# Streamed weights laid out tile by tile in memory, so that a load reads one 8 KB run per partition

## The chip, the core and the metric

The kernel runs on one core of a Trainium2 chip. A core has TensorE (matrix products; its weight loads are listed apart as PEld), VectorE (DVE), ScalarE (ACT), GpSimd (POOL) and SyncE (SP), which here only issues DMAs. Sixteen DMA engines move data between the chip's memory and the core's buffers (SBUF, 128 partitions). The metric is device microseconds from start to end of one launch. Laying out the inputs on the host is done before the launch and is not timed.

## What is computed

Four layers over 256 tokens of 1024 channels, all in float32. The first block has two layers: a mixer (hybrid of a gated recurrence and sparse attention, then latent attention) and an MLP with a gated side input. The second block has two layers: three mixers side by side (retention, RWKV-7, short convolution), then a mixture of 32 experts with two chosen per token. Cut to what matters for the weights:

```python
for i in range(2):                                   # first block
    m = hybrid_mixer(x, hy_w_in, ..., hy_w_out) if i == 0 else mla_mixer(x, mla_w_down, ..., mla_w_out)
    h = layer_norm(alpha * x + m)
    f = square(relu(h @ mlp_w1[i])) @ mlp_w2[i]
    e = sigmoid(h @ ple_w_gate[i]) * (p[i] @ ple_w_proj[i])
    x = layer_norm(alpha * h + f + e)
for l in range(2):                                   # second block
    x = x + gate1 * (mixers(modulate(rms_norm(x)), w_in[l], w_gate[l], w_branch[l]) @ w_o[l])
    x = x + gate2 * sum over the chosen experts e of
        weight[e] * ((silu(h @ w_exp_gate[l, e]) * (h @ w_exp_up[l, e])) @ w_exp_down[l, e])
```

An expert has three matrices: gate and up of 1024 x 512, down of 512 x 1024, 2 MB each. All 32 experts of a layer are read, 192 MB per layer.

## The kernel before

Activations lie with their channels on the partitions, 256 tokens along each. Weights stream through tiles of [128, 2048] float32, 1 MB, one DMA each. A dense tile is a block of `kc` times 128 rows and 2048 / `kc` columns; it is read by `wload` (L291 to L295) out of the matrix as it stands, so that each partition gets `kc` runs of 2048 / `kc` floats: 8 runs of 1 KB for most matrices, 4 of 2 KB or 2 of 4 KB for some. `wsplit` (L297 to L306) then copies half of such a tile into its high float32r part on ScalarE (L302) and forms the rest on VectorE or GpSimd (L305), and `mm3` makes three products of these parts (L318 to L320). `gemm_steps` runs a whole product so. The modulation weights w_ada are used as they come (L1091).

The experts (L1883 to L1902) use their matrices without parts. `xload` (L1730 to L1738) reads a matrix in two halves: gate and up in 4 runs of 2 KB per partition and half, down in 2 runs of 4 KB. Its tiles come in turn from three pools (`xtile`, L1720): 7 of the experts' ring (xw), the 7 of the dense weights (w) and 3 of a second ring, 17 in all; a load waits until the tile 17 loads earlier has been used. In step e the TensorE makes the gate product of expert e (L1758), the down product of expert e - 1 (L1782), the up product of e (L1758), adds the outputs of e - 1 to the tokens' sums (`combine`, L1923), then `choice` (L1746 on TensorE, L1749 on ScalarE, L1751 on VectorE) and `expert_act`: ScalarE L1765, VectorE L1767, two transposes L1770 on TensorE, VectorE L1772. The choice gives the weight that L1767 needs. Every fourth expert the tokens of four more experts are gathered (L1839). Behind the last expert all engines pass a branch (L1933), which is for expert lists of over 64 tokens.

All loads of weights are issued by SP in one queue, in an order that is fixed when the kernel is built, as is the order on each engine: a planner lays the instructions of the expert loop out by its own estimate of when each can start, except where the code has them in the written order (`ordered`, `manual_schedule`). At the start (L172 to L177) x and the first two weight tiles are loaded in turn: two parts of x in 1 KB runs, two halves of the first tile in runs of 512 bytes, the second tile in 1 KB runs.

Of the kernel before, what the change touches and what calls it, by code (L numbers as in the profile page):

```python
# [20 lines left out]
T = 256  # L21
# [5 lines left out]
# ---------------------------------------------------------------- host layout  # L27
# per-channel vectors, packed as columns of [128, n]
# [16 lines left out]
# shape constants, packed as columns of [128, n]  # L45
# [10 lines left out]
def constants():  # L56
# [23 lines left out]
    # block doubling of (I + A)^-1: rows t (partition), columns s; level b joins blocks of 2^b  # L80
# [10 lines left out]

def layout(a):
    """The arrays that the program reads, of the inputs: only moved, repeated and padded."""
# [4 lines left out]
    g["xT"] = a["x"][0].T  # L98
    g["pT"] = np.transpose(a["p"][:, 0], (0, 2, 1))
    w = a["hy_w_in"][0]  # L100
    xr, yr, q, k, v, iq, ik, iw = np.split(w, np.cumsum([512, 512, 512, 64, 64, 256, 64])[:7], axis=1)
    g["hy_w_in"] = np.concatenate(
        [iq, ik, ik, v, iw, np.zeros((1024, 60), np.float32), k, k, q, xr, yr], axis=1)
    for n in ("hy_ga_w", "hy_gx_w"):
# [5 lines left out]
    g["hy_w_out"] = a["hy_w_out"][0]  # L110
# [3 lines left out]
    g["mla_w_down"] = np.concatenate([w[:, 512:768], *[kr] * 4, *[krot] * 4, w[:, :512]], axis=1)  # L114
    w = a["mla_w_uq"][0].reshape(512, 16, 96)
    # the rotary parts of heads whose logits share a bank lie on the same partitions
# [4 lines left out]
    g["mla_w_uq"] = np.concatenate([x[:, i] for i in range(2) for x in (n, r, rot)], axis=1)  # L121
    w = a["mla_w_ukv"][0].reshape(256, 16, 128)
    g["mla_w_ukv"] = np.concatenate(
        [w[:, :, :64].reshape(256, 1024), w[:, :, 64:].reshape(256, 1024)], axis=1)
    g["mla_w_out"] = a["mla_w_out"][0]
    for n in ("mlp_w1", "mlp_w2", "ple_w_proj", "ple_w_gate"):
        g[n] = a[n]
# [3 lines left out]
    # four groups, four that are never chosen, the experts  # L131
# [4 lines left out]
    for n in ("w_ada", "w_in", "w_gate", "w_branch", "w_o", "w_exp_gate", "w_exp_up", "w_exp_down"):  # L136
        g[n] = a[n + "_2"]
# [17 lines left out]
class Prog:  # L155
    def __init__(self, ctx, tc, g, out):
# [13 lines left out]
        # x and the first weights in turn  # L170
        w, w1 = (self.wp.tile([128, 2048], FT, name="w", tag="w").rearrange("p (c n) -> p c n", c=8) for _ in range(2))
        self.first = [w, w1]  # L172
# [32 lines left out]
    def enter(self, phase):  # L205
        """The pools of a phase: products with parts of dense weights, or experts."""
# [63 lines left out]
    def t4(self, name, dt=FT, tag="t4"):  # L270
        """An activation of up to 1024 numbers in a partition."""
# [18 lines left out]
    # ---- products with streamed weights, three passes of exact float32r parts  # L290
    def wload(self, ap, k0, kc, c0, n):  # L291
        t = self.wp.tile([128, 2048], FT, name="w", tag="w")
        v = t[:, :kc * n].rearrange("p (c n) -> p c n", c=kc)
        self.nc.sync.dma_start(v, ap[k0:k0 + kc * 128, c0:c0 + n].rearrange("(c p) n -> p c n", p=128))
        return v  # L295

    def wsplit(self, v, kc, c0, n, fresh=False, pool=False):  # L297
        nc = self.nc
        src = v[:, :, c0:c0 + n]
        h = self.t4("fh", FR) if fresh else self.sp.tile([128, 1024], FR, name="wh", tag="wh")  # L300
        hv = h[:, :kc * n].rearrange("p (c n) -> p c n", c=kc)
        nc.scalar.activation(hv, src, AF.Copy)  # L302
        l = self.t4("fl", FR) if fresh else self.sp.tile([128, 1024], FR, name="wl", tag="wl")
        lv = l[:, :kc * n].rearrange("p (c n) -> p c n", c=kc)
# [3 lines left out]
    def split(self, src, h, l):  # L308
        """src = h + l in float32r parts; src may be in PSUM."""
# [3 lines left out]
    def mm3(self, out, wh, wl, wc, xh, xl, kc, x0=0, start=True, stop=True, ks=None):  # L313
        """out[128 columns wc.., T] += w^T x"""
# [11 lines left out]
    def gemm_steps(self, ap, kc, c0, nblk, x, evac, fresh=False, pool=(), first=None):  # L326
        """evac(j, n, bank) for each pair of blocks of 128 columns: bank[:, :n*T] = (x @ w)^T;
        fresh: x comes chunk by chunk, and the first pair of blocks takes each as it comes,
        after a first step that prepares this"""
        tb = 2048 // kc // 128  # L330
        xb = max(1, 1024 // kc // 128)
        for j in range(0, nblk, tb):
            nb = min(tb, nblk - j)
            v = first.pop(0) if first else self.wload(ap, 0, kc, c0 + j * 128, nb * 128)
            parts = {}
            for i in range(0, nb, 2):
                n = min(2, nb - i)
                if fresh and i + j == 0:
                    ws = [self.wsplit(v, kc, u * 128, 128, True) for u in range(2)]
# [9 lines left out]
                for u in range(n):  # L349
                    b = i + u  # L350
                    if b // xb not in parts:
                        w = min(xb, nb - b)
                        parts = {b // xb: self.wsplit(v, kc, b * 128, w * 128, pool=(j + b) % 4 in pool)}
# [29 lines left out]
    def beside(self, main, side):  # L383
        """the steps of side, between those of main, which yields how many units are to come; both results"""
# [34 lines left out]
    def rstd_tokens(self, sq, n, eps, fill=lambda n: None, units=0, out=None):  # L419
        """1 / sqrt(mean of n chunks + eps): [128 tokens, 2]"""  # L420
# [4 lines left out]
    def rstd_sums(self, sums, n, eps, out=None):  # L425
        """the same of what `partial` has summed in PSUM"""
# [14 lines left out]
    def by_token(self, r):  # L441
        """[128 tokens, 2] as [128, T] with all of it on every partition (in PSUM)"""
# [5 lines left out]
    def rstd(self, sq, n, eps, fill=lambda n: None, units=(0, 0)):  # L448
        """1 / sqrt(mean of n chunks + eps) by token, on every partition (in PSUM)"""
# [4 lines left out]
    def rms(self):  # L454
        """1 / rms(x) [128 tokens, 2]"""
# [51 lines left out]
    # ---- first block  # L507
# [11 lines left out]
    def softmax_pair(self, lg, n, scale, hs=2):  # L519
        """lg: PSUM [128, hs, n] logits / scale -> normalised P in SBUF [128, hs, n]"""  # L520
# [1595 lines left out]
```

## Time and profile before

| | |
|---|---|
| median of 3 runs | 2482.08 us (2476.62 to 2482.94) |
| span of the profiled execution | 2477.0 us; no other time of that execution is given |
| TensorE busy | 2295.0 us, 93% |
| VectorE, ScalarE, GpSimd busy | 46%, 35%, 8% |
| DMA | 658.71 MB in 409219 packets, mean 266 GB/s |
| packets under 2 KB, under 8 KB | 234544, 409008 |

A packet is one run that a DMA engine moves. Times are in microseconds from the start of the span unless marked ns. The page cuts the span into 40 equal slices of 61.9 us; a digit is a busy share in tenths. The DMA share is the packets' time over that of 16 engines; it passes 1 where the times of packets overlap. Waits are put down to what ended them.

### The profile page before, as it was taken

The numbers are of one execution on the slowest core, as the hardware profiler recorded it, in microseconds if no ns is written. First come the engines' busy times: TensorE is split into PE (matmuls) and PEld (weight loads), VectorE is DVE, ScalarE is ACT, GpSimd is POOL, SyncE is SP. The second block draws the span as 40 slices with busy tenths as digits, with TensorE's granted clock in tenths as the row PEclk, the third lists the DMA queues.
The fourth block names the chain that finished last, engine by engine and source line by source line (L and its number), as shares of the span: only waits on it lengthen the run. The fifth ranks groups of instructions, "written<-read, shape, count | busy, mean of one in ns | idle before, by whom it ended". The sixth has DMA issues, their size and how long they took to land. (4 is left out here: it accounts for less than half of the span.)

```text
span 2477.0 us, 45869 instructions
## 1 busy us (share of the span) xinstructions
PE 2295.0 (93%) x19846; PEld 1807.9 (73%) x19846; DVE 1144.9 (46%) x1864; ACT 869.2 (35%) x1415; POOL 200.2 (8%) x171
## 2 busy tenths in 40 slices
PE   7899999999999999989899988799999898998886
PEld 7689988799988898975555544389989755554443
DVE  6775566665555855652222211268556522222112
ACT  4654445554445434431111111253344411121111
POOL 6110000010001001010000000010011100000000
PEclk9999999999999999999999999999999999999998
DMA  8855565755567443569999999964335599999996
GB/s 275 266 186 187 181 209 198 238 172 187 181 203 243 151 134 112 184 241 363 394 393 393 394 394 394 366 213 154 121 121 195 204 374 394 394 393 394 394 394 254
DMA packets 409219, 658.71 MB, mean 266 GB/s; under 512 B 10416, under 2 KB 234544, under 8 KB 409008
## 3 DMA queue, kind: packets, MB, share of 16 engines
q1 hardware_dynamic: 407024, 652.14, 74.4%
q8 instruction: 159, 2.61, 0.4%
q10 hardware_dynamic: 1984, 3.54, 0.4%
q14 instruction: 52, 0.43, 0.0%
HBM read 654.59 MB, written 1.05 MB: 265 GB/s over the span
## 5 line engine op out<-in xcount | busy, mean ns | idle before, releaser
L302 ACT ACTIVATE wh<-w 128x1024 fp32r<-128x1024 f32 x359 | 380.4, 1060 | 561.7 <-PE bank L319 493.0
L305 DVE TENSOR_TENSOR wl<-w,wh 128x1024 fp32r<-128x1024 f32 x330 | 420.1, 1274 | 333.1 <-ACT wh L302 332.2
L318 PE MATMUL bank<-hh,wh 128*128 128x256 f32 x1568 | 454.3, 290 | 0.0
L320 PE MATMUL bank<-hh,wl 128*128 128x256 f32 x1568 | 444.4, 283 | 3.6 <-DVE wl L305 3.6
L319 PE MATMUL bank<-hl,wh 128*128 128x256 f32 x1568 | 444.0, 283 | 0.0
L318 PEld LDWEIGHTS bank<-hh,wh 128*128 128x128 f32 x1568 | 300.7, 192 | 11.2 <-issue 7.9
L1758 PE MATMUL bank<-xw,xg 128*64 128x256 f32 x2464 | 286.4, 382 | 21.6 <-DMA xw<-in_w_exp_up_dram 19.7
L320 PEld LDWEIGHTS bank<-hh,wl 128*128 128x128 f32 x1568 | 301.1, 192 | 5.0 <-DVE wl L305 5.0
L319 PEld LDWEIGHTS bank<-hl,wh 128*128 128x128 f32 x1568 | 301.2, 192 | 1.1 <-issue 1.0
L1758 PEld LDWEIGHTS bank<-xw,xg 128*64 128x64 f32 x2464 | 170.9, 137 | 136.8 <-DMA xw<-in_w_exp_up_dram 36.1
L1788 DVE TENSOR_TENSOR ey<-bank,ey 64x512 fp32r<-64x512 f32 x128 | 88.2, 689 | 263.3 <-ACT ey L1787 263.3
L1758 PE MATMUL bank<-w,xg 128*64 128x256 f32 x1632 | 191.1, 382 | 13.0 <-DMA w<-in_w_exp_up_dram 12.4
L1758 PEld LDWEIGHTS bank<-w,xg 128*64 128x64 f32 x1632 | 112.7, 137 | 89.5 <-DMA w<-in_w_exp_up_dram 23.4
L1787 ACT ACTIVATE ey<-bank 64x512 fp32r<-64x512 f32 x128 | 75.9, 593 | 268.2 <-PE bank L1782 220.5
L1751 DVE TENSOR_SCALAR ct<-cs 128x256 fp32r<-128x256 f32 x64 | 20.2, 316 | 324.0 <-ACT cs L1749 324.0
L1782 PE MATMUL bank<-xw,eh 128*64 128x512 f32 x608 | 143.6, 598 | 9.8 <-DMA xw<-in_w_exp_down_dram 8.6
L1749 ACT ACTIVATE cs<-bank 128x256 f32<-128x256 f32 x64 | 24.6, 384 | 363.3 <-PE bank L1746 363.3
L318 PE MATMUL bank<-rh,wh 128*128 128x256 f32 x512 | 144.9, 283 | 0.0
L319 PE MATMUL bank<-rl,wh 128*128 128x256 f32 x512 | 144.9, 283 | 0.0
L320 PE MATMUL bank<-rh,wl 128*128 128x256 f32 x512 | 144.9, 283 | 0.0
L1782 PE MATMUL bank<-w,eh 128*64 128x512 f32 x416 | 98.3, 598 | 9.7 <-DMA w<-in_w_exp_down_dram 9.6
L1824 POOL TENSOR_TENSOR woh<-oh,wt 128x256 f32<-128x256 f32 x64 | 37.5, 617 | 797.9 <-PE bank L1758 574.0
(526 smaller groups left out, 3871.0 us busy)
## 6 DMA issues: line engine op xcount, KB each, us to landing
xw<-in_w_exp_up_dram SPq DMA_DIRECT2D x78, 1024.0 KB, 15.5
xw<-in_w_exp_gate_dram SPq DMA_DIRECT2D x76, 1024.0 KB, 14.6
xw<-in_w_exp_down_dram SPq DMA_DIRECT2D x76, 1024.0 KB, 14.1
w<-in_mlp_w_dram SPq DMA_DIRECT2D x64, 1024.0 KB, 5.3
w<-in_w_exp_down_dram SPq DMA_DIRECT2D x52, 1024.0 KB, 14.1
w<-in_w_exp_gate_dram SPq DMA_DIRECT2D x52, 1024.0 KB, 14.4
w<-in_w_exp_up_dram SPq DMA_DIRECT2D x50, 1024.0 KB, 16.0
w<-in_w_ada_dram SPq DMA_DIRECT2D x48, 1024.0 KB, 5.4
```

The lines of the kernel that those rows point to most:

```text
L302: nc.scalar.activation(hv, src, AF.Copy)
L305: (nc.gpsimd if fresh or pool else nc.vector).tensor_tensor(lv, src, hv.bitcast(FT), op=OP.subtract)
L318: te.matmul(out, a, xh[x0 + k], start=start and k == 0, stop=False, skip_group_check=True)
L319: te.matmul(out, a, xl[x0 + k], start=False, stop=False, skip_group_check=True)
L320: te.matmul(out, b, xh[x0 + k], start=False, stop=stop and k == kc - 1, skip_group_check=True)
L1749: nc.scalar.activation(s, pc[:, :T], AF.Copy, accum_out=w)
L1751: nc.vector.tensor_scalar(ct, s, 0.0, None, op0=OP.not_equal)
L1758: self.nc.tensor.matmul(ps[64 * h:64 * h + 64, o:o + 256], xk(k), w(k)[:, h * 256:(h + 1) * 256], start=k == 0 and o == 0, stop=k == 7, sk ...
L1782: nc.tensor.matmul(py[64 * c:64 * c + 64], ht[:, b * 128 + h * 64:b * 128 + h * 64 + 64], wd(2 * h + b)[:, c * 512:(c + 1) * 512], start=n ...
L1787: nc.scalar.activation(y[:64, n], p, AF.Copy)
L1788: nc.vector.tensor_tensor(y[64:, n], p, y[:64, n].bitcast(FT), op=OP.subtract)
L1824: nc.gpsimd.tensor_tensor(woh[:, i, :, c], oh[:, i].bitcast(FT), wt[:, i, es, None].to_broadcast([128, G, 64]), op=OP.mult)
```

## The change

The host writes each streamed matrix as a sequence of tiles of [128, 2048], in the order of use, each row of a tile being what one partition receives. `tiled` does this for the matrices that are split into parts: a row holds the two halves of 1024 floats one behind the other, each half with its `kc` pieces of 1024 / `kc` columns. `rowwise` does it for those that are used as a whole tile (x, p, w_ada, the experts, two tiles of w_in). A load is then one contiguous run of 8 KB per partition and 1 MB in memory (x and the halves of the first tile: 4 KB runs). In the core, `halves` gives the two halves of a tile, `wsplit` takes a half that is contiguous, and the experts' tiles have the same arrangement as before. The arithmetic and its order, the tiles, the pools and the number of loads stay; comments are taken out.

```diff
+def tiled(w, kc):
+    w = np.asarray(w)
+    *lead, r, c = w.shape
+    n = 1024 // kc
+    w = np.concatenate([w, np.zeros((*lead, r, -c % (2 * n)), np.float32)], axis=-1)
+    w = w.reshape(*lead, r // (kc * 128), kc, 128, -1, 2, n)
+    d = len(lead)
+    return w.transpose(*range(d), d, d + 3, d + 2, d + 4, d + 1, d + 5).reshape(*lead, r // (kc * 128), -1, 128, 2048)
+
+def rowwise(w, kc, n):
+    w = np.asarray(w)
+    *lead, r, c = w.shape
+    w = w.reshape(*lead, r // (kc * 128), kc, 128, c // n, n)
+    d = len(lead)
+    return w.transpose(*range(d), d, d + 3, d + 2, d + 1, d + 4).reshape(*lead, r // (kc * 128), c // n, 128, kc * n)
...
-    g["xT"] = a["x"][0].T
+    g["xT"] = rowwise(a["x"][0].T, 4, T)[:, 0]
...
-    for n in ("w_ada", "w_in", "w_gate", "w_branch", "w_o", "w_exp_gate", "w_exp_up", "w_exp_down"):
-        g[n] = a[n + "_2"]
+    g["w_ada"] = rowwise(a["w_ada_2"], 8, 256)
+    w = tiled(a["w_in_2"], 8)
+    w[:, :, 4:6] = rowwise(np.asarray(a["w_in_2"])[:, :, 1024:1536], 8, 256)
+    g["w_in"] = w
+    for n, kc in (("w_gate", 8), ("w_branch", 4), ("w_o", 8)):
+        g[n] = tiled(a[n + "_2"], kc)
+    for n, kc in (("w_exp_gate", 4), ("w_exp_up", 4), ("w_exp_down", 2)):
+        g[n] = rowwise(a[n + "_2"], kc, 2048 // kc)[:, :, :, 0]
...
         for k, q in enumerate(self.x.q):
-            nc.sync.dma_start(q, g["xT"][k * 512:(k + 1) * 512].rearrange("(c p) t -> p c t", p=128))
-            n = slice(k * 128, k * 128 + 128)
-            nc.sync.dma_start(w[:, :, n], g["hy_w_in"][:, n].rearrange("(c p) n -> p c n", p=128))
-        nc.sync.dma_start(w1, g["hy_w_in"][:, 256:512].rearrange("(c p) n -> p c n", p=128))
+            nc.sync.dma_start(q.rearrange("p c t -> p (c t)"), g["xT"][k])
+            n = slice(k * 1024, k * 1024 + 1024)
+            nc.sync.dma_start(w[:, n], g["hy_w_in"][0, 0][:, n])
+        nc.sync.dma_start(w1, g["hy_w_in"][0, 1])
...
-    def wload(self, ap, k0, kc, c0, n):
+    def wload(self, ap, kc, row=0, col=0, n=2):
         t = self.wp.tile([128, 2048], FT, name="w", tag="w")
-        v = t[:, :kc * n].rearrange("p (c n) -> p c n", c=kc)
-        self.nc.sync.dma_start(v, ap[k0:k0 + kc * 128, c0:c0 + n].rearrange("(c p) n -> p c n", p=128))
-        return v
+        self.nc.sync.dma_start(t[:, :1024 * n], ap[row, col][:, :1024 * n])
+        return self.halves(t, kc)
...
-    def wsplit(self, v, kc, c0, n, fresh=False, pool=False):
-        src = v[:, :, c0:c0 + n]
+    def wsplit(self, src, kc, fresh=False, pool=False):
...
     def xload(self, ap, kc, n):
         half = []
         for h in range(2):
-            v = self.xtile().rearrange("p (c n) -> p c n", n=n)
-            rows = ap[h * kc * 64:(h + 1) * kc * 64]
-            self.nc.sync.dma_start(v, rows.rearrange("(c p) n -> p c n", p=128))
-            half.append(v)
+            t = self.xtile()
+            self.nc.sync.dma_start(t, ap[h])
+            half.append(t.rearrange("p (c n) -> p c n", n=n))
         return lambda k: half[k // (kc // 2)][:, k % (kc // 2)]
```

## Rows read from the trace of the kernel before

**Rows 1.** Page, the span in 40 slices: DMA busy tenths and rate
```profile
DMA  8855565755567443569999999964335599999996
GB/s 275 266 186 187 181 209 198 238 172 187 181 203 243 151 134 112 184 241 363 394 393 393 394 394 394 366 213 154 121 121 195 204 374 394 394 393 394 394 394 254
```

**Rows 2.** Stages: length, busy PE PEld DVE ACT POOL, clock, DMA share, GB/s
```profile
500.00:1000.00 500.00, 487.20 (x4886) 460.08 (x4884) 302.42 (x407) 230.47 (x302) 33.94 (x20) 0.99 0.53 170
1120.00:1587.00 467.00, 425.74 (x3102) 244.64 (x3099) 99.25 (x195) 79.17 (x187) 16.41 (x28) 1.00 1.04 393
1985.00:2450.00 465.00, 422.46 (x3086) 241.70 (x3084) 99.07 (x194) 78.52 (x185) 16.41 (x28) 1.00 1.04 393
```

**Rows 3.** TensorE groups, 1120 to 1587: busy, mean ns, idle before and its ends
```profile
L1758 PE MATMUL bank<-xw,xg 128*64 128x256 f32 x1194 | 139.1, 382 | 11.6 <-DMA xw<-in_w_exp_up_dram 11.3
...
L1782 PE MATMUL bank<-xw,eh 128*64 128x512 f32 x288 | 68.1, 598 | 4.3 <-DMA xw<-in_w_exp_down_dram 4.3
```

**Rows 4.** Timeline of TensorE, one transpose row per expert: start, length, [idle before]
```profile
1185.10 0.44 PE L1770 MATMUL bank<-con,em 128*128 128x128 f32 x2 [1.47 <-DVE em L1767]
...
1244.35 0.33 PE L1770 MATMUL bank<-con,em 128*128 128x128 f32 x1 [1.47 <-DVE em L1767]
1258.12 0.44 PE L1770 MATMUL bank<-con,em 128*128 128x128 f32 x2 [1.47 <-DVE em L1767]
...
1299.47 0.44 PE L1770 MATMUL bank<-con,em 128*128 128x128 f32 x2
...
1353.33 0.33 PE L1770 MATMUL bank<-con,em 128*128 128x128 f32 x1
1365.84 0.33 PE L1770 MATMUL bank<-con,em 128*128 128x128 f32 x1
...
1507.77 0.44 PE L1770 MATMUL bank<-con,em 128*128 128x128 f32 x2
...
1571.50 0.44 PE L1770 MATMUL bank<-con,em 128*128 128x128 f32 x2
1587.40 0.44 PE L1770 MATMUL bank<-con,em 128*128 128x128 f32 x2
...
2229.47 0.44 PE L1770 MATMUL bank<-con,em 128*128 128x128 f32 x2
...
2452.67 0.33 PE L1770 MATMUL bank<-con,em 128*128 128x128 f32 x1
```

**Rows 5.** Timeline of TensorE, the choice's products of two experts
```profile
1150.08 0.38 PE L1746 MATMUL bank<-con,woh 128*128 128x128 f32 x2
...
1276.32 0.44 PE L1746 MATMUL bank<-con,woh 128*128 128x128 f32 x2
```

**Rows 6.** DMA packets from 484 to 494, 1370 to 1376, 1365 to 1366 us
```profile
DMA packets 3443, 3.49 MB, mean 349 GB/s; under 512 B 51, under 2 KB 3442, under 8 KB 3442
...
DMA packets 1159, 2.32 MB, mean 387 GB/s; under 512 B 33, under 2 KB 33, under 8 KB 1158
...
DMA packets 106, 0.41 MB, mean 414 GB/s; under 512 B 5, under 2 KB 5, under 8 KB 106
```

**Rows 7.** DMA queue 14 in 0.1 us from 1992.7 and 1321.8: packets, MB, share
```profile
q14 instruction: 1, 0.01, 19.3%
...
q14 instruction: 1, 0.01, 26.2%
```

**Rows 8.** Timeline of SP's queue, from 1105 us: two loads issued
```profile
1105.41 12.47 SPq L1736 DMA_DIRECT2D xw<-in_w_exp_gate_dram  x2
```

**Rows 9.** Timeline: waits outside the expert stretches
```profile
12.90 1.06 ACT L302 ACTIVATE wh<-w 128x1024 fp32r<-128x1024 f32 x1 [1.93 <-DMA w<-in_hy_w_in_dram]
...
101.92 0.42 PE L1091 MATMUL bank<-w,silc 128*32 128x256 f32 x4 [2.45 <-DMA w<-in_w_ada_dram]
...
1607.27 0.66 PE L445 MATMUL bank<-con,rstd 128*128 128x128 f32 x2 [6.92 <-PEq L1933]
```

**Rows 10.** All copies of line L302: duration ns min/median/max, first and last start
```profile
L302 ACT ACTIVATE wh<-w x359: 1039/1061/1070, 6.6 to 1954.7; 128x1024 fp32r<-128x1024 f32 x180
```

More of the change, by code (lines that the diff above doesn't have):

```diff
@@ L120, in layout @@
     n = w[:, :, :64].reshape(512, 2, 512)
-    g["mla_w_uq"] = np.concatenate([x[:, i] for i in range(2) for x in (n, r, rot)], axis=1)
+    g["mla_w_uq"] = tiled(np.concatenate([x[:, i] for i in range(2) for x in (n, r, rot)], axis=1), 4)
     w = a["mla_w_ukv"][0].reshape(256, 16, 128)
[L123 to L127, printed above, removed]
+    g["mla_w_ukv"] = tiled(np.concatenate(
+        [w[:, :, :64].reshape(256, 1024), w[:, :, 64:].reshape(256, 1024)], axis=1), 2)
+    g["mla_w_out"] = tiled(a["mla_w_out"][0], 8)
+    for n, kc in (("mlp_w1", 8), ("mlp_w2", 8), ("ple_w_proj", 2), ("ple_w_gate", 8)):
+        g[n] = tiled(a[n], kc)
     g["pos"] = np.asarray(a["positions_2"]).reshape(1, T).astype(np.int32)
@@ L169, in __init__ @@
         nc.scalar.activation(junk, junk, AF.Copy)
-        w, w1 = (self.wp.tile([128, 2048], FT, name="w", tag="w").rearrange("p (c n) -> p c n", c=8) for _ in range(2))
-        self.first = [w, w1]
+        w, w1 = (self.wp.tile([128, 2048], FT, name="w", tag="w") for _ in range(2))
+        self.first = [self.halves(w, 8), self.halves(w1, 8)]
         for k, q in enumerate(self.x.q):
-            nc.sync.dma_start(q, g["xT"][k * 512:(k + 1) * 512].rearrange("(c p) t -> p c t", p=128))
-            n = slice(k * 128, k * 128 + 128)
-            nc.sync.dma_start(w[:, :, n], g["hy_w_in"][:, n].rearrange("(c p) n -> p c n", p=128))
-        nc.sync.dma_start(w1, g["hy_w_in"][:, 256:512].rearrange("(c p) n -> p c n", p=128))
+            nc.sync.dma_start(q.rearrange("p c t -> p (c t)"), g["xT"][k])
+            n = slice(k * 1024, k * 1024 + 1024)
+            nc.sync.dma_start(w[:, n], g["hy_w_in"][0, 0][:, n])
+        nc.sync.dma_start(w1, g["hy_w_in"][0, 1])
         self.phase = self.right = self.ring = None
@@ L288, in act, with halves @@
         return Act([self.q4(f"{name}{k}", dt, tag) for k in range(n // 4)])
-    def wload(self, ap, k0, kc, c0, n):
+    @staticmethod
+    def halves(t, kc):
+        return [t[:, 1024 * h:1024 * h + 1024].rearrange("p (c n) -> p c n", c=kc) for h in range(2)]
+    def wload(self, ap, kc, row=0, col=0, n=2):
         t = self.wp.tile([128, 2048], FT, name="w", tag="w")
-        v = t[:, :kc * n].rearrange("p (c n) -> p c n", c=kc)
-        self.nc.sync.dma_start(v, ap[k0:k0 + kc * 128, c0:c0 + n].rearrange("(c p) n -> p c n", p=128))
-        return v
-    def wsplit(self, v, kc, c0, n, fresh=False, pool=False):
+        self.nc.sync.dma_start(t[:, :1024 * n], ap[row, col][:, :1024 * n])
+        return self.halves(t, kc)
+    def wsplit(self, src, kc, fresh=False, pool=False):
         nc = self.nc
-        src = v[:, :, c0:c0 + n]
         h = self.t4("fh", FR) if fresh else self.sp.tile([128, 1024], FR, name="wh", tag="wh")
-        hv = h[:, :kc * n].rearrange("p (c n) -> p c n", c=kc)
+        hv = h.rearrange("p (c n) -> p c n", c=kc)
         nc.scalar.activation(hv, src, AF.Copy)
         l = self.t4("fl", FR) if fresh else self.sp.tile([128, 1024], FR, name="wl", tag="wl")
-        lv = l[:, :kc * n].rearrange("p (c n) -> p c n", c=kc)
+        lv = l.rearrange("p (c n) -> p c n", c=kc)
         (nc.gpsimd if fresh or pool else nc.vector).tensor_tensor(lv, src, hv.bitcast(FT), op=OP.subtract)
@@ L333, in gemm_steps @@
             nb = min(tb, nblk - j)
-            v = first.pop(0) if first else self.wload(ap, 0, kc, c0 + j * 128, nb * 128)
+            v = first.pop(0) if first else self.wload(ap, kc, 0, c0 * kc // 2048 + j // tb, -(-nb // xb))
             parts = {}
@@ L338, in gemm_steps @@
                 if fresh and i + j == 0:
-                    ws = [self.wsplit(v, kc, u * 128, 128, True) for u in range(2)]
+                    ws = [self.wsplit(v[u], kc, True) for u in range(2)]
                     yield 0
@@ L351, in gemm_steps @@
                     if b // xb not in parts:
-                        w = min(xb, nb - b)
-                        parts = {b // xb: self.wsplit(v, kc, b * 128, w * 128, pool=(j + b) % 4 in pool)}
+                        parts = {b // xb: self.wsplit(v[b // xb], kc, pool=(j + b) % 4 in pool)}
                     wh, wl = parts[b // xb]
@@ L929, in ple_parts @@
         ptl = self.t2("ptl", FR).rearrange("p (c t) -> p c t", c=2)
-        w = self.wload(self.g["ple_w_proj"][i], 0, 2, 0, 1024)
+        w = self.wload(self.g["ple_w_proj"][i], 2)
         self.split(pt, pth, ptl)
         ws = []
-        for n in (0, 512):
+        for half in w:
             h, l = (self.t4("pw", FR).rearrange("p (c n) -> p c n", c=2) for _ in range(2))
-            self.split(w[:, :, n:n + 512], h, l)
+            self.split(half, h, l)
             ws.append((h, l))
@@ L995, in second @@
             for half in range(4):
-                v = self.wload(g["mlp_w2"][i], q * 1024, 8, half * 256, 256)
+                v = self.wload(g["mlp_w2"][i], 8, q, half)
                 for b in range(2):
                     j = half * 2 + b
-                    wh, wl = self.wsplit(v, 8, b * 128, 128)
+                    wh, wl = self.wsplit(v[b], 8)
                     self.mm3(acc[j // 2][:, (j % 2) * T:(j % 2 + 1) * T], wh, wl, 0, rh, rl, 8,
@@ L1081, in ada_halves @@
         for q in range(24 * L):
-            w = self.wload(self.g["w_ada"][q // 24], 0, 8, q % 24 * 256, 256)
+            w = self.wp.tile([128, 2048], FT, name="w", tag="w")
+            self.nc.sync.dma_start(w, self.g["w_ada"][q // 24, 0, q % 24])
+            w = w.rearrange("p (c n) -> p c n", c=8)
             if self.ada_sums and q - self.ada_sums[0] == 16:
@@ L1510, in retention @@
         for j in range(2):
-            w = self.wload(g["w_in"][l], 0, 8, 1024 + j * 256, 256)
+            w = self.wload(g["w_in"][l], 4, 0, 4 + j)
             for h in range(2):
-                wh, wl = self.wsplit(w[:, 4 * h:4 * h + 4], 4, 0, 256)
+                wh, wl = self.wsplit(w[h], 4)
                 for i in range(2):
@@ L1941, in crowded @@
                         w = self.ring.tile([128, 2048], FT, name="xw", tag="xw").rearrange("p (c n) -> p c n", c=kc)
-                        rows = g[n][l, bass.ds(e, 1), h * kc * 128:(h + 1) * kc * 128]
-                        nc.sync.dma_start(w, rows.rearrange("e (c p) n -> p (e c) n", p=128))
+                        rows = g[n][l, bass.ds(e, 1), h]
+                        nc.sync.dma_start(w, rows.rearrange("e p (c n) -> p (e c) n", c=kc))
                         half.append(w)
```

16 lines of the change are left out of this document (8 added, 8 removed).

## The prediction

> **What bounds the kernel now.** I read the profile from the coarse to the fine. First the page's forty slices [rows 1]: the DMA line is full in two plateaus, slices 18 to 25 and 32 to 39, and well below full elsewhere. Then the table of stages [rows 2]: in the dense stretch from 500 to 1000 us TensorE is busy for 487.20 of 500.00 us while the DMA engines are busy for 0.53 of it. In the two expert stretches (one per layer) the share is 1.04, the rate 393 GB/s, and TensorE has idle time: 41.3 us in the first, 42.5 us in the second. Those two stretches are 932 us of the 2477.0.
>
> What ends TensorE's idle time there is the landing of an expert's matrix: 11.6 us before the matmuls of one buffer kind and 4.3 us before those of the down matrices, and two more groups like them [rows 3]. The transposes L1770 come once per expert and so give the pace [rows 4]. From 1507.77 to 1571.50 us four experts took 63.73 us, 15.93 each: 6 loads of 1 MB at 393 GB/s are 16.0. From 1299.47 to 1353.33 us, with loads still in stock, four took 53.86, 13.47 each: TensorE's own pace. Earlier still it was slower: 1185.10 to 1244.35 us is 59.25, 14.81 each. The cause is an order: at 1150.08 us the choice (L1746) stands behind the combine, so its chain over ScalarE and VectorE holds the transposes by 1.47 us (brackets of the rows of 1185.10 to 1258.12); at 1276.32 us it stands between the halves of the down product, and that wait is gone [rows 5]. So each layer runs on stock at TensorE's pace until about expert 17 (1365.84 and 2229.47 us) and on the loads' pace from there to expert 31 (1587.40 and 2452.67 us) [rows 4].
>
> **The loads: what a longer run is worth.** Three stretches with packets of one size give the rate by run length [rows 6]: 349 GB/s at 1 KB, 387 at 2 KB, 414 at 4 KB (one microsecond only). For a load of 1 MB (1.0486 million bytes) that is 3.005, 2.710 and 2.533 us. The whole expert stretch, two thirds 2 KB and one third 4 KB, runs at 393, 2.668 us a load; taking the 2 KB loads out leaves 2.584 for 4 KB. Each of 16 engines moves 64 KB of a load: 64, 32 or 16 packets. From 64 to 32 the load falls by 0.295 us, 9.2 ns per packet; by that price 16 packets give 2.563 (inside 2.533 to 2.584), and 8 packets of 8 KB give 2.489. I take 2.50 us, 419 GB/s. The bounds: the data part alone with no cost per packet, 3.005 minus 64 times 9.2 ns, is 2.416; at the other end the rate stops rising at 2.563. No 8 KB packet of the weight queue is in the trace; the only ones are instruction loads of queue 14, of which two are shown [rows 7]: 19.3% of 16 engines in 0.1 us is 309 ns, 26.2% is 419 ns. Eight of the first are 2.47 us, of the second 3.35. I go by the weight queue's own three points, which are nearer in kind, and keep 419 ns for the slow side.
>
> **The expert stages, step by step.** Layer 0: 393 GB/s for 467 us [rows 2] are 183.5 MB, 175 loads. At 2.668 minus 2.50 us each that is 29.4 us off the last landing, so expert 31's transposes would come at 1558.0 instead of 1587.40. TensorE alone, from 1365.84 with 14 experts at 13.47, could reach them at 1554.4. The loads therefore still end last, by 3.6 us, and this is the point at which the gain would stop. Two things take a little off the 29.4: the first 17 loads go to free buffers before TensorE begins the stage (SP issues the last of these and the next one around 1105.41) [rows 8], and every later one waits until the load 17 places ahead is used up, so in the early, slow part the loads can run only as far ahead as TensorE lets them. Following load by load (landing 2.52 us behind the last or 4.5 after its buffer is free, used at landing or at TensorE's pace) leaves 26.3 us in layer 0 and 27.1 in layer 1, whose TensorE floor is 2229.47 plus 188.6, so 2418.1 against 2452.67. Sum 53.4, taken as 54 with the stray gaps shrinking too.
>
> **The rest.** The first block's weights and x: ScalarE waits 1.93 us for the second weight tile [rows 9]; the two megabytes before it come in runs of 0.5 and 1 KB and will come in 4 KB runs. Bounds 0, if the parts that GpSimd makes of each tile hold the products anyway, and the whole 1.93; I take 1.5, as two loads at 3.005 become two at 2.56 and a third shrinks by 0.5. In the dense stages one exposed load is left, 2.45 us before the w_ada products [rows 9]: its data part shrinks from 3.005 to 2.50, so 0.5. All other dense loads land under matmuls (TensorE 97% busy in the dense stretch); nothing there is late next but TensorE itself, and if the cover were gone a load of 1 MB would show its 2.5 us. The copies that split a tile now read a contiguous block instead of 8, 4 or 2 runs: 359 of them, of all those forms, lie between 1039 and 1070 ns [rows 10], so at most 0.02 us each and off the path; zero. Instruction counts on the five engines do not change; a load is one DMA before and after, on SP as before, and no wait is added. SP's issue stands still for several microseconds when the queue is full (12.47 us for two in rows 8, waits included); with a quarter as many packets it will stand less, which lets no load begin before its buffer is free. One thing can go either way: behind the experts of layer 0 TensorE stands 6.92 us at the branch of L1933 while w_in streams [rows 9]. If that is the fetch of instructions, it shares engines with the data, and larger packets ahead of it, or a queue that is empty sooner, could move it. I take 0 and bound it by half of it either way, 3.5 us.
>
> Sum: 54 + 1.5 + 0.5 = 56 us. The profiled execution's span is 2477.0 and gives 2421.0; the runs shown are 2476.62 to 2482.94 with the median 5.1 us above that span, so the predicted median is 2482.1 - 56 = 2426 us.
>
> [...] The rows show the rate rising from 349 to 387 to 414 GB/s between 1 and 4 KB [rows 6]. [...]
>
> **The rivals.**
> - *TensorE becomes the bound.* Loads at 2.45 us or less. Then the gain per layer stops at 1587.40 - 1554.4 = 33.0 and 2452.67 - 2418.1 = 34.6; with 2 for the rest 70 us, 2412. For it: the floor is only 3.6 us away.
> - *The rate has flattened.* 8 KB runs move like 4 KB ones, 2.563 us: 175 times 0.105 is 18.4 us per layer, less 2 us as above, 33 in all, 2447 with 1.5 for the rest. For it: 0.295 us was gained by the first doubling and about 0.15 by the second, and the long packets are unseen.
> - *Nothing changes* because run length is not what sets the pace: 2482. Against it: the 4 KB loads run faster in the same stretch.
> - *The order stays slow.* The order of the choice was made at build time and may depend on how late the loads were thought to be. If L1746 stays behind the combine throughout, TensorE keeps 14.81 per expert: from 1244.35 five groups of four and three more experts (13.77 each, by the 1258.12 row) reach 1581.9, and the gain is 5.5 us in layer 0, the same again in layer 1 and 2 for the rest, 2469 in all. It decides from three experts later than now (3.6 over 1.34 us per expert).
> - *Slower: long packets collide.* Sixteen engines each hold an 8 KB run, and a packet takes over 331 ns. That is the break-even (8 times 331 plus about 20 ns is 2.668). At 345 ns, between the two of rows 7 and nearer to the shorter, a load takes 2.78, 175 times 0.11 is 19 us per layer: 2520.
>
> **How the numbers follow.** Forecast 0.60; TensorE bound 0.07; flattened 0.09; slow order 0.10, of which about half within 0.3%; nothing 0.05; collide 0.09. What a measurement of this kernel can tell from no change is about 0.3%, 7.4 us. Faster by more than that: 0.60 + 0.07 + 0.09 + 0.06 = 0.82; within it 0.04 + 0.05 = 0.09; slower 0.09. The range goes from the floor case with the first block's whole 1.93 us, 2411, to the slow order, 2470, and leaves out the two cases behind it, 0.14 together, and a little at either end.
>
> **What would show it.** Right: the rate of the expert stretches near 419 GB/s with 8 KB packets; four experts in the late part near 60 us (24 loads of 2.50) instead of 63.73; TensorE's waits for the expert matrices still there but shorter; expert 31 of layer 0 near 1559. Wrong: waits for matrices gone (TensorE bound), a rate of 406 (flattened) or under 393 (collide), L1746 behind L1923 after the tenth expert (order).

## The result

The changed kernel takes 2427.57 us (median; 2423.36 to 2428.28) against 2482.51 for the kernel before (2476.62 to 2483.17), 54.9 us less. The ratio is 0.9778, with a 95% interval from 0.9763 to 0.9793. The profiled execution has a span of 2426.2 us and took 2428.05. The forecast was 2426.

By line, operation and tile the instructions of every engine stand in the order of before. So only times have moved, and the two traces can be laid over each other instruction by instruction.

The page of the changed kernel, the span in 40 slices (DMA busy in tenths, rate) and the packet counts:

```profile
DMA  7745555555556534367999999955333679999996
GB/s 267 297 161 176 190 200 208 194 208 190 177 189 236 207 123 131 108 266 281 420 420 420 420 420 420 417 194 178 135 120 127 258 320 420 420 420 420 420 420 260
DMA packets 93315, 658.71 MB, mean 272 GB/s; under 512 B 10416, under 2 KB 11824, under 8 KB 14128
q1 hardware_dynamic: 91376, 652.14, 69.3%
```

The two plateaus of [rows 1] are still there, at 420 instead of 394 GB/s; the bytes are the same. The table of stages of the changed kernel (length, busy PE PEld DVE ACT POOL, clock, DMA share, GB/s):

```profile
500.00:1000.00 500.00, 487.18 (x4871) 460.34 (x4870) 302.10 (x404) 229.44 (x300) 34.89 (x21) 0.99 0.49 171
...
1130.00:1350.00 220.00, 205.53 (x1546) 123.88 (x1548) 51.34 (x102) 38.65 (x91) 9.39 (x16) 1.00 1.01 419
1350.00:1520.00 170.00, 169.09 (x1249) 98.65 (x1246) 39.74 (x77) 32.93 (x76) 6.98 (x12) 1.00 1.01 420
```

Against [rows 2] the dense stretch is the same work in the same time, with the DMA share down from 0.53 to 0.49. In the expert stretch the line is full all the way, and from 1350 to 1520 us TensorE now has 0.9 us of idle time in 170. The waits of TensorE in the expert stretch of layer 0 (groups as in [rows 3]: busy, mean ns, idle before and what ended it):

```profile
L1792 PE MATMUL bank<-xw,xg 128*64 128x256 f32 x1232 | 141.2, 381 | 1.2 <-SPq L1967 1.1
L1792 PE MATMUL bank<-w,xg 128*64 128x256 f32 x816 | 94.2, 381 | 2.5 <-DMA w<-in_w_exp_up_dram 2.5
L1816 PE MATMUL bank<-xw,eh 128*64 128x512 f32 x288 | 68.0, 597 | 0.6 <-DMA xw<-in_w_exp_down_dram 0.5
L1816 PE MATMUL bank<-w,eh 128*64 128x512 f32 x208 | 49.0, 597 | 0.3 <-DMA w<-in_w_exp_down_dram 0.2
...
L1804 PE MATMUL bank<-con,em 128*128 128x128 f32 x64 | 14.0, 300 | 15.5 <-DVE em L1801 15.5
```

The 11.6 us that TensorE waited for one kind of buffer (xw) are 1.2, and 4.3 for the down matrices are 0.6. The 1.1 put down to SP (SyncE, which stands at the branch by then) are two waits that end as loads of an up matrix land, at 1558.77 and 1561.26 us. Before, the two groups that read the dense weights' buffers (w) waited as well:

```profile
L1758 PE MATMUL bank<-w,xg 128*64 128x256 f32 x816 | 95.4, 382 | 5.8 <-DMA w<-in_w_exp_up_dram 5.5
L1782 PE MATMUL bank<-w,eh 128*64 128x512 f32 x208 | 49.2, 598 | 4.1 <-DMA w<-in_w_exp_down_dram 3.9
```

The four groups together waited 25.8 us before and wait 4.6 now. What is left as the largest idle group is the wait behind the choice in the first experts (15.5 us, the same before), mostly 1.47 us each as in [rows 4]. The transposes, one row per expert (L1804 here, L1770 in [rows 4]):

```profile
1130.56 0.33 PE L1804 MATMUL bank<-con,em 128*128 128x128 f32 x1 [1.36 <-DVE em L1801]
...
1370.52 0.33 PE L1804 MATMUL bank<-con,em 128*128 128x128 f32 x1
...
1490.76 0.33 PE L1804 MATMUL bank<-con,em 128*128 128x128 f32 x1
...
1504.63 0.33 PE L1804 MATMUL bank<-con,em 128*128 128x128 f32 x1
...
1564.32 0.33 PE L1804 MATMUL bank<-con,em 128*128 128x128 f32 x1
...
2206.61 0.33 PE L1804 MATMUL bank<-con,em 128*128 128x128 f32 x1
...
2401.84 0.33 PE L1804 MATMUL bank<-con,em 128*128 128x128 f32 x1
```

From expert 17 (1370.52) to expert 26 (1490.76) TensorE now runs at its own pace; before, it fell behind from expert 18 on. The step after that, of 13.86 us, is 1.35 above its own pace, and the last four, 1504.63 to 1564.32, are at the loads' pace: 59.69 us.

Laid over each other, the difference is made of four pieces. The first transposes of layer 0 come 6.2 us later than before (1130.56 against 1124.39 in the trace of before). From there to expert 31 layer 0 gains 29.3 us (433.76 us instead of 463.01). Between the layers 0.2 is lost. Layer 1 gains 28.0 (1966.73 to 2401.84, 435.11 us, instead of 463.08). 29.3 + 28.0 - 6.2 - 0.2 = 50.9, and the spans differ by 50.8. (Of the 29.3, the waits for loads shown above account for 21.2; the rest lies in TensorE's busy time between the first transposes and the last, 423.10 us before and 415.10 now. Why that is shorter stays open, but for 1.5 us of lower clock that come up again below.) So the two expert stages alone are worth 57 us, and the 6 us lost ahead of them need a cause of their own.

### The profile page after: what moved, and what is told of

Same layout as the page of the kernel before. It is cut to its first block, busy times and chain, and to the rows that moved or that the text cites. A ratio compares the mean times of both kernels' runs of the same rounds, so it can differ in the third digit from the quotient of the medians.

```text
span 2426.2 us, 45869 instructions
## 1 busy us (share of the span) xinstructions
PE 2287.1 (94%) x19846; PEld 1816.3 (75%) x19846; DVE 1146.2 (47%) x1864; ACT 868.7 (36%) x1415; POOL 200.3 (8%) x171
```

## The experiments

The theory: each packet costs about 9 ns on top of the data, whatever its length; the experts' loads set the end of both expert stages; all other loads lie under TensorE's work. The rivals: the rate is flat above 4 KB and the gain is something else; the dense tiles bring part of it, or cost the 6 us; TensorE's order or its own pace is the bound.

### The loads alone

The kernel holds nothing but loads (and a copy of x), in one run length after the other; it was run once:

```python
for s in (1, 2, 4, 8, 16, 1, 0):           # runs per partition and load; 0: one run of 16 KB
    for k in range(12):
        w = wp.tile([128, 2, 2048], FT, name="w", tag="w")
        ...
            nc.sync.dma_start(w[:, h].rearrange("p (s n) -> p s n", s=s),
                              ap[e % 64, h].rearrange("(s a) (b n) -> (a b) s n", s=s, b=s))
```

> The weight loads alone: 24 loads of 1 MB each in runs of 8, 4, 2, 1, 0.5 and again 8 KB, then 12 of 2 MB in runs of 16 KB, into 12 buffers of 8 KB per partition, no compute (the output is only a copy of x). Theory A (a fixed cost of about 9.2 ns per packet on top of 2.416 us of data): 2.49, 2.56, 2.71, 3.005, 3.59 and 2.49 us per MB, 2.45 per MB at 16 KB. Rival (the rate has flattened and the last step has another cause): 4, 8 and 16 KB all alike. Rival (the loads are held up by TensorE's reads or by other traffic): every size faster here than in the kernels, 8 KB at 2.41 us or less.

Its stretches, in the order 8, 4, 2, 1, 0.5, 8 and 16 KB (length, busy POOL, clock, DMA share, GB/s):

```profile
20.00:60.00 40.00, 0.00 (x0) 1.00 1.01 421
75.00:120.00 45.00, 0.00 (x0) 1.00 1.03 409
137.00:185.00 48.00, 0.00 (x0) 1.00 1.05 387
200.00:260.00 60.00, 0.00 (x0) 1.00 1.10 348
270.00:345.00 75.00, 0.00 (x0) 1.00 1.06 290
360.00:410.00 50.00, 0.00 (x0) 1.00 1.01 422
425.00:470.00 45.00, 0.00 (x0) 1.00 1.00 425
```

The steps from landing to landing are finer than the whole GB/s: 2.484, 2.560, 2.711, 3.01 and 3.614 us per MB, 2.485 again, and 2.449 at 16 KB (428 GB/s; the edges of the last stretch make 425 of it). From 128 packets per engine to 8 the load falls by 1.13 us, so a packet costs 9.4 ns, and what is left without packets comes to 2.409 us, 435 GB/s (an estimate from these two sizes). With these two numbers the sizes between come out as 2.559, 2.710 and 3.011, and 16 KB as 2.446. The first theory stands; the rate isn't flat, at 8 KB or above. Nor does the issue set it: SyncE's issue of one load lasts 0.33 us with 8 KB runs and mostly 2.36 us with 4 KB runs, and the price of a packet is the same across that jump (9.5 ns from 8 to 16 packets, 9.4 from 16 to 32). Inside the kernels the longest issue of an expert load was 7.10 us before and is 0.65 in the changed kernel. TensorE is idle in the run of the loads alone, and a load of 8 KB runs is only about 1% faster than in the kernel (2.504 to 2.515 us), so the last rival named there, a hold-up by TensorE, has next to nothing to explain.

### Experts alone, and all others alone

The first kernel takes the kernel before and changes the experts' matrices only:

```diff
-            v = self.xtile().rearrange("p (c n) -> p c n", n=n)
-            rows = ap[h * kc * 64:(h + 1) * kc * 64]
-            self.nc.sync.dma_start(v, rows.rearrange("(c p) n -> p c n", p=128))
-            half.append(v)
+            t = self.xtile()
+            self.nc.sync.dma_start(t, ap[h])
+            half.append(t.rearrange("p (c n) -> p c n", n=n))
```

> Only the experts' matrices are laid out tile by tile; every other weight is loaded in rows as before. Theory A (the whole gain comes from the experts' loads, every other load was hidden): the two expert stretches shrink by 29 and 28 us as in the changed kernel, 1 MB loads at 2.49 us, so about 2482.5 - 57 = 2425 us, within 4 us of the changed kernel (2427.6). Rival B (the dense tiles bring part of the gain, by an earlier start or earlier prefetch): about 2440 or more. Rival C (the dense tiles cost the 6 us that the dense part lost in the changed kernel's profile, at TensorE's lower clock): the dense part has none of these four steps and the median is 3 to 6 us below the changed kernel's, 2421 to 2424; if the steps come by chance from run to run, the median is that of the changed kernel within 2 us.

It takes 2423.63 us (2420.02 to 2427.85), ratio 0.977 (0.9757 to 0.9783): the whole gain of the change.

The second is its counterpart, the changed kernel with these lines turned back.

> All weights but the experts' are laid out tile by tile; the experts' matrices are loaded in rows of 2 and 4 KB as before. Theory A: no dense load bounds the end, so 2482 us within 3 us (ratio 0.999 to 1.001), the expert stretches at 393 GB/s. Rival B: 2470 or less. Rival C (the dense tiles move TensorE's waits so that its clock falls for longer): 2486 to 2489, with the low-clock steps near 105, 140, 395 and 1115 us in the trace.

2483.07 us (2480.34 to 2485.55), ratio 1.0006 (0.9996 to 1.0016). All the other tiles together bring nothing that can be measured: by the interval, between 1 us of gain and 4 us of cost. Theory A holds in both kernels; B is out.

The first kernel's median lies in the range that rival C named, the second's does not. The traces say more. The 6.2 us of the changed kernel are, for the most part, four short stretches where the same matmuls take longer with no wait in between: 1.55 us from 103.7, 1.34 from 142, 1.44 from 394 and 1.40 from 1113 us on. Another 0.4 of the kind lies at 34 us. In each the granted clock is at its lower level, 0.50, for longer (6.83 us from 103.61 and from 1113.95 us, 3.41 before), or falls where it stayed up before (to 0.50 for 3.41 us from 144.57 and from 397.15 us); at 34 us it comes back up at 35.34 instead of 34.16 us. TensorE's waits just ahead are nearly the same in three of the four: 1.98 us at 141 us before and at 143.6 now, 1.03 ahead of the third, 3.92 and 3.90 ahead of the fourth. The first and the second of them (length, busy PE PEld DVE ACT POOL, clock, DMA share, GB/s), before:

```profile
104.00:109.00 5.00, 5.00 (x41) 3.09 (x41) 2.29 (x7) 1.26 (x6) 0.00 (x0) 0.82 1.07 380
140.00:146.00 6.00, 4.97 (x37) 4.36 (x38) 4.93 (x8) 2.11 (x5) 0.00 (x0) 1.00 0.84 275
```

the changed kernel:

```profile
104.00:109.00 5.00, 4.58 (x24) 2.55 (x24) 2.17 (x6) 1.56 (x6) 0.00 (x0) 0.50 1.01 424
140.00:146.00 6.00, 4.02 (x30) 2.67 (x29) 3.83 (x7) 2.31 (x3) 0.00 (x0) 0.88 0.63 235
```

and the kernel with only the experts' tiles, whose dense part is that of before, instruction by instruction and load by load:

```profile
104.00:109.00 5.00, 5.00 (x30) 2.64 (x26) 1.57 (x4) 0.77 (x2) 0.00 (x0) 0.53 1.06 379
140.00:146.00 6.00, 4.03 (x20) 3.31 (x19) 4.24 (x6) 1.37 (x3) 0.00 (x0) 0.74 0.76 247
```

The clock is at its lower level, 0.50, for all of the first stretch in the changed kernel, and nearly so with the old dense loads (0.53). Three of the four steps are in that kernel too (1.54, 1.34 and 1.40 us, not the one at 394), and three in the kernel with only the dense tiles (not the one at 1113). So the steps do not need the dense tiles: they differ between two executions of the same dense part, and the profiled execution of before had fewer of them. Whether the dense tiles make them more frequent stays open. Layer 0's first transposes come between 1128.0 and 1131.0 us in the traces of all eight kernels with dense tiles, at 1128.83 in the kernel without them, whose profiled execution is the slowest of its five, and at 1124.39 before; the medians leave room for some 4 us. Fifteen runs of the kernel before, made beside these two, lie between 2474.99 and 2486.93, a spread as long as some eight such steps. What decides on a step in one execution stays open.

### Runs of 4 KB and of 1 KB inside the kernel

```diff
-            self.nc.sync.dma_start(t, ap[h])
+            self.nc.sync.dma_start(t.rearrange("p (s n) -> p s n", s=2), ap[h].rearrange("s p n -> p s n"))
```

(and s=8 in the second; the host lays the experts out to match). TensorE's order is that of the changed kernel in both.

> The changed kernel, but all experts' matrices in two runs of 4 KB per partition instead of one of 8 KB (16 packets per engine and load instead of 8). By the loads measured alone, 2.56 instead of 2.484 us each: 175 loads per layer, 13.3 us later per layer, 2427.6 + 27 = 2454 us, loads landing every 2.56 us in the kernel. Rival (above 4 KB nothing more is gained inside the kernel, and the changed kernel's gain had another cause, such as fewer packets to issue): 2428 us.

2448.96 us (2447.93 to 2450.03), ratio 0.9863 (0.9847 to 0.988).

> The changed kernel, but all experts' matrices in eight runs of 1 KB per partition. By the loads measured alone 3.01 us each: 175 times 0.524 is 92 us per layer, about 2611 us, TensorE waiting for loads from the first experts on. Rival (the loads' price inside the kernel is not that of the loads alone, since TensorE's reads or a gap at the issue come on top): off this by more than 10 us.

2603.22 us (2602.63 to 2604.67), ratio 1.0487 (1.0469 to 1.0504). They are 5 and 8 us short of the sums. The 4 KB kernel is far from its rival's 2428; the 1 KB kernel stays inside the 10 us that its rival set, and on the side of the shorter time. From the landing of a layer's load 17 to its load 191 the 4 KB kernel takes 450.6 us in either layer and the 1 KB kernel 527.4 and 527.3, against 437.7 and 439.0 in the changed kernel. That is 24.6 and 178.1 us for both layers, where 26.6 and 183.4 were summed: the 8 KB loads run some 20 to 30 ns above their price alone inside the kernel (2.504 and 2.514 us over the last 91 loads of the two layers, against 2.484), the 1 KB loads less than 10 (3.02 against 3.01). That is 2.0 and 5.3 us of the 5 and 8; the other 2 to 3 us lie outside these stretches.

### TensorE's floor, and what it depends on

To see TensorE's own pace, half of each down matrix was left out of the loads:

```diff
-            self.nc.sync.dma_start(t, ap[h])
+            m = 1024 if kc == 4 else 2048
+            self.nc.sync.dma_start(t[:, :m], ap[h][:, :m])
...
-        return lambda k: half[k // (kc // 2)][:, k % (kc // 2)]
+        return lambda k: half[k // (kc // 2)][:, 0 if kc == 4 else k % (kc // 2)]
```

> The changed kernel, but only half of each down matrix is loaded and that half is used twice (the output is then another; every matmul stays). Theory (TensorE's own pace is the floor, and it lies some 7 us below in layer 0 and 9 us in layer 1, read from the steps of 12.51 and 16.33 us per expert): loads of an expert take 12.5 us against 13.47 of TensorE, no waits for them after the first experts, about 2428 - 16 = 2412 us. Rival (something else than the experts' loads sets the last experts' pace): 2420 or more. Rival (fewer loads make TensorE itself faster): below 2405.

2476.1 us (2473.25 to 2477.75): with a sixth of the experts' bytes gone it is 48.5 us slower than the changed kernel. The theory's 2412 is far off; the time lies in the open range of the first rival (2420 or more), which didn't say what else would set the pace. The timeline of TensorE late in layer 0 shows why (L1793 gate and up, L1958 combine, L1781 choice, L1805 transposes):

```profile
1526.80 1.47 PE L1793 MATMUL bank<-w,xg 128*64 128x256 f32 x12
1528.19 1.22 PE L1958 MATMUL bank<-ct,ey 128*128 128x256 f32 x8
1529.25 0.38 PE L1781 MATMUL bank<-con,woh 128*128 128x128 f32 x2
1531.45 0.33 PE L1805 MATMUL bank<-con,em 128*128 128x128 f32 x1 [1.82 <-DVE em L1802]
```

The choice stands behind the combine at this late expert too, as in the first ten of the changed kernel. With fewer bytes to load, the order made at build time came out otherwise, and this is the prediction's rival of the slow order, met in a kernel where no one had asked for it. It says nothing on the floor. Three kernels with the order written out by hand take the two things apart. The first passes no `between` and has the choice behind the combine; the other two pass it, and the third also loads only half of each down matrix:

```diff
         for n in range(4):
+            if n == 2 and between:
+                between()                  # the choice of the next expert
...
+            with self.tc.manual_schedule(engines={ENG.PE}):
```

> The changed kernel with the choice's products behind the combine for every expert, by hand, and all loads whole. Theory (in the kernel with half of each down matrix that order alone made the time, not the loads): TensorE at 14.81 us per expert in four, so the same 2476 us within 5, and no waits for loads at the end of a layer. By the prediction's own rival 2469 in the scale of before. Rival (the half matrices cost something of their own): 2455 or less here.

2478.66 us (2475.62 to 2480.86), ratio 0.9981 (0.9972 to 0.9991): the order alone makes that time, with all loads whole. TensorE shows no wait for an expert's matrix in layer 0, only 45.2 us behind the choice:

```profile
L1818 PE MATMUL bank<-xw,eh 128*64 128x512 f32 x272 | 61.6, 592 | 0.0
L1818 PE MATMUL bank<-w,eh 128*64 128x512 f32 x192 | 43.6, 592 | 0.0
L1804 PE MATMUL bank<-con,em 128*128 128x128 f32 x58 | 12.7, 300 | 45.2 <-DVE em L1801 45.2
```

> The changed kernel with the choice's products written by hand between the halves of the down product for every expert, where the changed kernel has them only from about the eleventh expert of a layer on (all loads whole). Theory (from the first experts on the load line is full, so the last landing sets the end, and TensorE's slow first ten experts cost only the little that buffers come free late): 0 to 5 us less, 2422 to 2428 us. Rival (TensorE's early pace still counts in full): ten experts times 1.47 us in each layer, 2400 us or less.

2425.03 us (2422.65 to 2427.04), ratio 0.977 (0.9753 to 0.9787): with the choice early from the first expert on it can't be told from the changed kernel. From 1130 to 1350 us TensorE has no idle time left, where the changed kernel had 14.5, and the line carries what it carried:

```profile
1130.00:1350.00 220.00, 220.00 (x1632) 129.37 (x1630) 52.29 (x104) 42.05 (x98) 9.31 (x16) 1.00 1.01 420
```

TensorE then meets the loads from expert 19 on instead of 27, and the last matrix of layer 0 lands 437.8 us behind load 17, as in the changed kernel (437.7).

> As the run with the order by hand between the halves, and with only half of each down matrix loaded (the half is used twice, so the output is another; every matmul stays). Theory (TensorE's own pace is then the bound, 24 steps of 12.51 and 7 of 16.33 us from the first transposes to the last of a layer, 414.5 us against 433.8 and 435.1 in the changed kernel): 40 us less, 2388 us, no waits for expert matrices. Rival (loads still decide): 2400 or more.

2382.42 us (2380.57 to 2385.07), ratio 0.9595 (0.9579 to 0.9611), 45 us below the changed kernel, where 40 were expected. From 1130 to 1560 us no group of TensorE's waits for a load; the groups of gate and up, and the transposes:

```profile
L1793 PE MATMUL bank<-xw,xg 128*64 128x256 f32 x1168 | 133.8, 381 | 0.0
L1793 PE MATMUL bank<-w,xg 128*64 128x256 f32 x816 | 93.7, 381 | 0.0
...
L1805 PE MATMUL bank<-con,em 128*128 128x128 f32 x64 | 14.0, 300 | 1.4 <-DVE em L1802 1.4
```

The two expert stages give 39.4 (414.6 us in layer 0 from the first transposes to the last), and 3.5 more lie between the layers: 398.9 us from the last transposes of layer 0 to the first of layer 1, instead of 402.4. So TensorE's floor with the early choice is some 40 us below the changed kernel. Its steps there are 12.51 us, and 16.33 once in four experts, 13.4 in the mean; six loads take 14.9 to 15.1. In the changed kernel the experts' loads are still the bound.

## Why the prediction was right

*The reading of the stage.* The landing of experts' matrices ended 25.8 of the 41.3 us of TensorE's idle time in layer 0, not all of it; the other 15.5 are the waits behind the choice, which the change leaves as they were.

*The price of a load.* 2.50 us was taken and 2.484 measured alone, 2.51 in the kernel; the 9.2 ns per packet, read from three rates of [rows 6], are 9.4. The step from a mixed 2.668 to 2.50 was 0.168 per load. Measured over loads 17 to 191 of layer 0 it is 2.684 to 2.515, again 0.168. Both ends of it lie 0.02 to 0.03 us above the loads alone (2.661 for the mix of before, by the prices measured alone, and 2.484). Of the two 8 KB packets of queue 14 [rows 7] the shorter, 309 ns, is near the 313 ns (median) of the weight queue's own; the longer, 419 ns, was rightly set aside.

*The sum for the two expert stages* was 53.4, taken as 54; it is 57.2. The term that was mis-sized is the deduction: 29.4 was worked out for the last landing and cut to 26.3 and 27.1, since the loads could run only as far ahead as TensorE lets them in its slow part. They gained 29.3 and 28.0. The line is full from 1130 us on (419 GB/s, share 1.01) in spite of TensorE's slow order, and with a faster TensorE in that part the last landing comes no sooner. No deduction was due in layer 0, and at most 1.4 in layer 1.

*TensorE's floor* was put 3.6 us ahead of the loads in layer 0. From 1490.76 on TensorE's own steps (12.51, 16.33 and then three of 12.51) would end at 1557.1 instead of 1564.32, so it is 7.2. Of the 3.6 us between, 2.0 come from the mean of 13.47 used for 14 experts: only three steps of 16.33 lie in them, not three and a half. Another 1.5 are one early step of 19.06 us (from 1166.04, [rows 4] show its end at 1185.10), in which the granted clock was 0.91 before (0.50 from 1167.39 to 1170.80 us); now it takes 17.60, at 1.00. The gain stood on the safe side of that point, and the rival "TensorE becomes the bound" was further away than thought.

*The start* was given 1.5 us and brought none. ScalarE's wait for the second weight tile fell from 1.93 to 1.42 us, and the products did not come sooner: the first matmul starts at 7.90 instead of 7.70. This was the bound at zero, and the term should have been taken there.

*The wait before the w_ada products* was given 0.5 us. It fell by 1.33, and all of it came back behind it (changed kernel):

```profile
101.29 1.07 PE L1126 MATMUL bank<-w,silc 128*32 128x256 f32 x16 [1.12 <-DMA w<-in_w_ada_dram]
104.42 0.69 PE L587 MATMUL bank<-pta,vt 128*64 128x256 f32 x2 [2.06 <-DVE pta L580]
```

The same products waited for VectorE's copy for 0.30 us before, in this row of the kernel before:

```profile
103.72 0.69 PE L554 MATMUL bank<-pta,vt 128*64 128x256 f32 x2 [0.30 <-DVE pta L547]
```

The copy itself began 0.68 us later (103.58 against 102.90). VectorE's chain was the next to be late, and the prediction didn't look for it. Against a sum of 56, these two terms are 2 us that were not there, and the expert stages 3 us more than was taken.

*The branch* behind layer 0 was taken as unchanged, within 3.5 us, and is nearly so (6.92 us in [rows 9]); the changed kernel, and then the kernel with the slow order, where the last expert load had landed 43 us before this row instead of 17:

```profile
1583.79 0.66 PE L478 MATMUL bank<-con,rstd 128*128 128x128 f32 x2 [6.54 <-PEq L1967]
```

```profile
1609.73 0.45 PE L478 MATMUL bank<-con,rstd 128*128 128x128 f32 x1 [4.17 <-PEq L1973]
```

In the floor kernel it is 4.04. In these two kernels, and in the one with half of each down matrix (4.13), the layer's last load landed 43 to 46 us before this row; in the seven others it landed 17 to 18 us before, and the wait is 6.2 to 6.9. So this wait is some 2.4 us shorter where the layer's loads end well ahead of it, which the prediction held possible. That it is a fetch of instructions behind data is argued, not shown. In the changed kernel the last expert is still at the loads' pace, and the wait stays.

*The signs named in advance.* The rate is 420 GB/s with 8 KB packets (419 forecast); the last four steps of layer 0 take 59.69 us (60); the waits are there but shorter; expert 31 of layer 0 comes at 1564.32, which is 1558.2 after taking off the 6.2 us that it starts late (1558.0 worked out for the loads, 1559 named). The choice stands between the halves of the down product from the same expert as in [rows 5]:

```profile
1279.18 1.89 PE L1816 MATMUL bank<-xw,eh 128*64 128x512 f32 x8
1281.00 0.44 PE L1780 MATMUL bank<-con,woh 128*128 128x128 f32 x2
1281.37 1.94 PE L1816 MATMUL bank<-xw,eh 128*64 128x512 f32 x8
```

*The rivals.* Flattened at 4 KB was priced at 2447; the kernel with all experts at 4 KB takes 2449, so the price was right and the premise wrong. The slow order did not come, but it is real: priced at 2469, it takes 2478.66 when it is made by hand. The working took 14.81 us per expert; in that kernel four of the five groups of four from expert 8 to 28 of layer 0 take 60.7 to 61.0 us, since the expert that carries the gather takes 19.08 rather than 17.60 us in them. The clock makes the difference; two such steps of that kernel, layout as in the table of stages:

```profile
1290.35:1309.43 19.08, 17.61 (x125) 12.38 (x125) 5.33 (x11) 4.20 (x9) 0.48 (x1) 0.91 1.01 416
1412.06:1429.66 17.60, 16.13 (x124) 10.93 (x124) 5.34 (x11) 4.20 (x9) 0.48 (x1) 1.00 1.01 421
```

The work is the same, and in the first the granted clock is 0.91: at its lower level for a part of it, right behind TensorE's wait for the choice (1.82 us). There are four such steps in layer 0 and three in layer 1, 10.4 us in all, about what the price was short by (9.7). Long packets do not collide: 313 ns against the break-even of 331.

*What was not foreseen* is the 6 us of lower clock in the profiled execution. The sum was made against the profiled execution of before and then moved to the median by a constant 5.1 us. Wherever a run has both, its time is 1.8 us above its span; so about 3.3 of the 5.1 say that this one execution was faster than the median. The clock steps that it lacked would do that, which is argued and not shown. The two profiled executions differ by 50.8 and the medians by 54.9. That the forecast came within 2 us owes something to luck: two small terms that were not there (2.0) and expert stages sized 3.2 too low nearly cancel, 57 for the experts and nothing else against the 56 summed.

## What to carry to other kernels

Where the DMA line is full, price a load by its packets: here 2.409 us per MB and 9.4 ns for each packet of one engine, from 0.5 to 16 KB. A layout on the host that makes one run per partition is worth that price times the packets saved, and only in the stages where the line sets the end: all of the dense tiles brought nothing. When the size of loads changes, compare the order of the instructions too: an order planned at build time can move with it, and here that was worth about 50 us, nearly as much as the change, some 10 of them by the lower clock behind the longer waits.

## What the runs showed of the hardware

- A load's price is linear in its packets over the whole range measured, 0.5 to 16 KB per run, within 0.003 us (one execution), and what is left without packets comes to 2.409 us per MB, 435 GB/s, an estimate from these loads. At 16 KB it is another 1.4% faster than at 8 KB.
- The loads are hardly slower beside a busy TensorE: 2.484 us alone, 2.504 to 2.515 in the expert stages.
- TensorE's granted clock, after waits of 1.0 to 3.9 us, falls to the lower level (0.50) in one execution and not in another of the same instructions (0.74 and 1.00 from 140 to 146 us, with only the experts' tiles and before), or stays there longer (6.83 us instead of 3.41, in the changed kernel and before); each such difference is 1.3 to 1.6 us here. Some eight of them would make the spread of the fifteen runs; that they do is not shown, since each kernel has one trace.
- In the kernel with the slow order short waits cost twice: seven of the waits of 1.8 us behind the choice are followed by a stretch of lower clock (0.91 over the step from 1290.35 us) that costs 1.5 us more.
